# Giving each unit of split weights in the first MLP its own start address in SBUF

## The chip, the cores and the metric

The kernel runs on one core of a Trainium2 chip. The metric is the device time of one execution in microseconds (us). The kernel before took 1201.2, 1201.91 and 1201.94 us in three runs; the median is 1201.91 us.

## The reference

The program is a decoder trunk of two layers over 512 tokens of width 1024, in float32. Each layer is a mixer followed by a dense MLP with a hidden width of 4096:

```python
for layer in range(DEPTH):                      # DEPTH = 2
    h = rmsnorm(x, norm_mix_g[layer])
    mix = even_mixer(h, ...) if layer % 2 == 0 else mlstm_mixer(h, ...)
    x = x + mix
    h = rmsnorm(x, norm_mlp_g[layer])
    x = x + sqrelu_mlp(h, mlp_w1[layer], mlp_w2[layer])

def sqrelu_mlp(h, w1, w2):
    return jnp.square(jax.nn.relu(h @ w1)) @ w2
```

The even mixer runs a state-space layer beside a dilated attention; the odd one is an mLSTM in chunks. This document is about the MLP of layer 0.

## The kernel before, in words

Activations stand transposed: 128 channels on the partitions, 512 tokens along a row. Every large weight matrix is cut into units of 128 x 1024 floats: eight blocks of 128 x 128 that stand side by side in a row of 4096 bytes. A unit passes through three steps. A DMA puts it into a raw buffer `wr` (three of these). `w_pump` (line 151) then splits it: ScalarE copies it to `wh` rounded to the type fp32r (line 158), and VectorE writes the rest, raw minus `wh`, to `wl` (line 159). There are two buffers of each in the pool `wp`, and from the first MLP on a third in the pool `wp2`; units take them in turn (lines 154 to 157). Activations are split in the same way into a high and a low part, so that a product becomes three matmuls that add up in PSUM (`mm3`, line 174): `wh` with the high part, `wh` with the low part, `wl` with the high part. In each of them a 128 x 128 block of the weights is the stationary operand, which LDWEIGHTS puts into the array, and 512 columns of activations are the moving one. So a unit is worth 24 pairs of LDWEIGHTS and matmul.

The first MLP (`mlp`, line 261) uses 64 units, that is 1536 matmuls: in two halves, 16 units of `w1` (moving: the eight high and eight low tiles of `hg`) and then 16 of `w2` (moving: the tiles `sh` and `sl`, two units for one output). The order of the units is the list that `unit_list` makes (line 1272); splits are made two units ahead, in the MLP three (line 153). The second MLP (`mlp_rows`) is another function, with units of its own.

Addresses: a pool lays its buffers one after the other along a partition's row, and pools follow one another. In the program as it is allocated, all buffers of `wh` and `wl`, the buffer of `hg` and all of `sh` and `sl` start at 96 more than a multiple of 256 bytes, and since blocks are 512 bytes and tiles 2048 bytes long, so does every operand of the first MLP's products. Two other products take the weights from the same `wh` and `wl` with moving tiles that start elsewhere. In the output projection of the odd mixer (line 1227) these are `mh` and `ml`, which all start at 160 more than a multiple of 256, 64 bytes off the weights. In that of the even mixer (line 1001) they are the four 4096-byte tiles `y` at 96, and `yh` and `yl` at 224, 128 bytes off; the order of line 34 mixes the two kinds, three matmuls of one block at a time, in the order y, yh, yh, y, y, yh, y, yh of a unit's blocks.

Of the kernel before, what the change touches and what calls it, by code (L numbers as in the profile page):

```python
# [10 lines left out]
F32R = mybir.dt.float32r  # L11
# [5 lines left out]
P = 128  # L17
# [44 lines left out]
class Trunk:  # L62
# [88 lines left out]
    def w_pump(self):  # L151
        n = 0 if self.wp2 is None else 1
        self.w_dma(min(self.wi + self.AHEAD_DMA + n * self.MORE_DMA, len(self.units)))
        while self.wsx < min(self.wi + self.AHEAD_SPLIT + n, len(self.units)):
            r = self.raw.pop(self.wsx)
            third = self.wp2 is not None and self.wsx % 3 == 2
            pool, bufs = (self.wp2, 1) if third else (self.wp, 2)
            h = self.t(pool, (P, 1024), "wh", F32R, bufs)
            l = self.t(pool, (P, 1024), "wl", F32R, bufs)
            self.copy_act(h, r)  # L160
            self.sub(l, r, h.bitcast(F32))
            self.split[self.wsx] = (h, l)
            self.wsx += 1
# [97 lines left out]
    def mlp(self, nxt):  # L261
        with self.tc.tile_pool(name="mp", bufs=1) as mp:
            for half in range(2):
                s = []
                for m in range(16):
                    z = self.proj(self.hg)
                    if half == 0 and m == 1:
                        r2 = self.norm_finish_sq()
                    rr = self.tmp("rr")
                    self.act(rr, z, AF.Relu)  # L270
                    sh = self.t(mp, (P, T), f"sh{m}", F32R)
                    sl = self.t(mp, (P, T), f"sl{m}", F32R)
                    self.act(sh, rr, AF.Square)
                    sf = self.tmp("sf")
                    self.mul(sf, rr, z)
                    self.sub(sl, sf, sh.bitcast(F32))
                    s.append((sh, sl))
                for m in range(KT):
                    o = self.proj(s, first=True, last=False, ks=range(0, 8))
                    self.proj(s, acc=o, first=False, last=True, ks=range(8, 16))  # L280
                    e = self.tmp("ev", bufs=3)
                    self.mul(e, o, r2)
                    self.add(self.x[m], self.x[m], e)
                    if half == 1:
                        self.prep(m, nxt)
# [989 lines left out]
    def unit_list(self):  # L1275
        a = self.a
        units = []
        for step in EVEN_SEQ.split():
            if step[0] in "uvab":
                n = int(step[1])  # L1280
                i = {"u": n, "v": 12 + n, "a": 4 + 2 * (n % 2) + 4 * (n // 2), "b": 5 + 2 * (n % 2) + 4 * (n // 2)}[step[0]]
                units.append(a["w_l0"][i])
        units += [a["w_l0"][i] for i in range(16, 26)]
        mlp = lambda l: [a["w1"][l, h * 16 + m] if ph == 0 else a["w2"][h, m] for h in range(2) for ph in range(2) for m in range(16)]
        units += mlp(0)
        base = {"z": 0, "v": 1, "q": 9, "k": 17, "o": 25}
        units += [a["w_l1"][base[step[0]] + int(step[1:])] for step in ODD_SEQ.split() if step[0] in base]
        units += [a["w_l1"][33 + m] for m in range(8)]
        units += self.rows_units()
        return units  # L1290
# [114 lines left out]
```

## Time and profile before

| what | value |
|---|---|
| median of three runs | 1201.91 us |
| profiled execution | 1202.68 us |
| its span, first to last instruction | 1200.9 us |
| TensorE (PE) busy | 1177.3 us, 98% |
| weight loads (PEld) busy | 968.8 us, 81% |
| VectorE (DVE) busy | 736.8 us, 61% |
| ScalarE (ACT) busy | 574.4 us, 48% |
| GpSimd (POOL) busy | 65.4 us, 5% |
| granted TensorE clock | 0.996 |

The profiled execution is 0.77 us longer than the median; its span leaves 1.8 us of it outside the first and last instruction. Matmuls are pipelined: a matmul's row lasts 0.39 us, while the next one starts after 0.23 us, so that the durations overlap and the busy time of PE says little. What a matmul costs is read from the distance of starts. In a timeline the columns are start (us), duration (us), engine, line, operation, names (output, then inputs), the shape, and how many follow each other in the row.

### The profile page before, as it was taken

The numbers are of one execution on the slowest core, as the hardware profiler recorded it, in microseconds if no ns is written. First come the engines' busy times: TensorE is split into PE (matmuls) and PEld (weight loads), VectorE is DVE, ScalarE is ACT, GpSimd is POOL, SyncE is SP. The second block draws the span as 40 slices with busy tenths as digits, with TensorE's granted clock in tenths as the row PEclk, the third lists the DMA queues.
The fourth block names the chain that finished last, engine by engine and source line by source line (L and its number), as shares of the span: only waits on it lengthen the run. The fifth ranks groups of instructions, "written<-read, shape, count | busy, mean of one in ns | idle before, by whom it ended". The sixth has DMA issues, their size and how long they took to land.

```text
span 1200.9 us, 15231 instructions
## 1 busy us (share of the span) xinstructions
PE 1177.3 (98%) x5580; PEld 968.8 (81%) x5580; DVE 736.8 (61%) x1307; ACT 574.4 (48%) x1009; POOL 65.4 (5%) x122
## 2 busy tenths in 40 slices
PE   6989999999999999999999999999999999999998
PEld 5868776788888888888888888887888888888887
DVE  8799864554443344435449773874665564477796
ACT  5467777443432133423336554454344344466664
POOL 0522220000000000000010000000000000000000
PEclk9989999999999999999999999999999999999999
DMA  6434522333323333232334333321499995346664
GB/s 233 123 89 124 144 75 62 114 106 94 100 91 102 101 93 104 90 104 89 103 95 152 105 106 106 93 75 45 164 350 365 349 344 176 118 148 195 206 189 157
DMA packets 61196, 170.41 MB, mean 142 GB/s; under 512 B 15481, under 2 KB 16585, under 8 KB 61121
## 3 DMA queue, kind: packets, MB, share of 16 engines
q1 hardware_dynamic: 59904, 168.13, 42.9%
q0 software_dynamic: 1216, 1.31, 0.5%
q8 instruction: 44, 0.72, 0.3%
q14 instruction: 32, 0.25, 0.1%
HBM read 145.78 MB, written 21.53 MB: 139 GB/s over the span
## 4 chain that ended last, share of the span: by engine, by line
PE 93%; DVE 3%; ACT 2%; POOL 1%; issue 1%; DMA 0%; SPq 0%; DVEq 0%; ACTq 0%
PE acc L123 83%; PE psa L123 5%; PE psb L123 3%; DVE wl L96 1%; PE psb L902 1%; POOL rA L547 1%; ACT wh L120 0%; ACT hg L117 0%; DMA wr<-in_w_l 0%; DVE hg L108 0%; PE psb L1212 0%; PE psb L307 0%; DVE x L96 0%; DVE CG L96 0%; PE psb L653 0%
## 5 line engine op out<-in xcount | busy, mean ns | idle before, releaser
L123 PE MATMUL acc<-hg,wh 128*128 128x512 f32 x1616 | 505.8, 393 | 8.9 <-ACT hg L117 8.2
L120 ACT ACTIVATE wh<-wr 128x1024 fp32r<-128x1024 f32 x219 | 231.9, 1060 | 492.0 <-PE acc L123 401.1
L96 DVE TENSOR_TENSOR wl<-wr,wh 128x1024 fp32r<-128x1024 f32 x219 | 268.2, 1226 | 269.1 <-ACT wh L120 268.5
L123 PEld LDWEIGHTS acc<-hg,wh 128*128 128x128 f32 x1616 | 302.4, 189 | 70.8 <-ACT hg L117 8.2
L123 PE MATMUL acc<-hg,wl 128*128 128x512 f32 x808 | 316.8, 392 | 0.6 <-DVE wl L96 0.6
L123 PEld LDWEIGHTS acc<-hg,wl 128*128 128x128 f32 x808 | 152.3, 188 | 32.4 <-DVE wl L96 1.1
L123 PE MATMUL acc<-wh,sp 128*128 128x512 f32 x384 | 111.4, 389 | 0.0
L123 PE MATMUL acc<-sh,wh 128*128 128x512 f32 x256 | 99.6, 389 | 0.0
L123 PE MATMUL acc<-sl,wh 128*128 128x512 f32 x256 | 99.6, 389 | 0.0
L123 PE MATMUL acc<-sh,wl 128*128 128x512 f32 x256 | 99.6, 389 | 0.0
L123 PEld LDWEIGHTS acc<-wh,sp 128*128 128x128 f32 x384 | 72.1, 188 | 15.0
L123 PE MATMUL acc<-wh,hg 128*128 128x512 f32 x192 | 63.2, 404 | 5.5 <-ACT wh L120 5.5
L123 PE MATMUL acc<-wl,sp 128*128 128x512 f32 x192 | 67.9, 390 | 0.4 <-DVE wl L96 0.4
L123 PEld LDWEIGHTS acc<-sl,wh 128*128 128x128 f32 x256 | 48.0, 188 | 10.1
L123 PEld LDWEIGHTS acc<-sh,wl 128*128 128x128 f32 x256 | 48.0, 188 | 9.9
L123 PEld LDWEIGHTS acc<-sh,wh 128*128 128x128 f32 x256 | 48.0, 188 | 9.9
L96 DVE TENSOR_TENSOR tq<-tq,tq 128x1024 f32<-128x1024 f32 x32 | 39.1, 1223 | 20.1 <-DMA tq<-in_w2s 19.7
L123 PEld LDWEIGHTS acc<-wh,hg 128*128 128x128 f32 x192 | 37.0, 194 | 13.4 <-ACT wh L120 5.9
L120 ACT ACTIVATE sp<-s 128x256 fp32r<-128x256 f32 x112 | 44.6, 408 | 1.9 <-PE acc L123 1.3
L96 DVE TENSOR_TENSOR ev<-acc,r 128x512 f32<-128x512 f32 x16 | 11.1, 692 | 53.3 <-PE acc L123 53.3
L96 DVE TENSOR_TENSOR sp<-s,sp 128x256 fp32r<-128x256 f32 x112 | 43.5, 418 | 0.3 <-ACT sp L120 0.3
L123 PEld LDWEIGHTS acc<-wl,sp 128*128 128x128 f32 x192 | 36.0, 188 | 8.2 <-DVE wl L96 0.8
(318 smaller groups left out, 1491.5 us busy)
## 6 DMA issues: line engine op xcount, KB each, us to landing
wr<-in_w SPq DMA_DIRECT2D x96, 512.0 KB, 3.5
wr<-in_w_l SPq DMA_DIRECT2D x67, 512.0 KB, 3.5
tq<-in_w2s SPq DMA_DIRECT2D x32, 512.0 KB, 6.3
T<-tq SPq DMA_DIRECT2D x32, 512.0 KB, 5.0
wr<-T SPq DMA_DIRECT2D x32, 512.0 KB, 3.4
wr<-in_w2s SPq DMA_DIRECT2D x24, 512.0 KB, 4.0
x<-in_xT SPq DMA_DIRECT2D x16, 256.0 KB, 4.7
na<-scr SPq DMA_DIRECT2D x8, 256.0 KB, 4.3
```

What stands on the lines that cost most here:

```text
L96: return self.nc.vector.tensor_tensor(out=o, in0=x, in1=y, op=op)
L120: return self.nc.scalar.activation(o, x, AF.Copy)
L123: return self.nc.tensor.matmul(o, l, r, start=start, stop=stop)
L547: gt = lambda o, x, y, op: self.nc.gpsimd.tensor_tensor(out=o, in0=x, in1=y, op=op)
L902: self.nc.tensor.transpose(t[:, k * P:(k + 1) * P], p[:, k * P:(k + 1) * P], self.ident)
```

## The change

Each of the 64 units of the first MLP gets an offset of 5 times its number, modulo 64, in elements; that is 0, 20, 40, ... bytes modulo 256, so that every multiple of 4 bytes from 0 to 252 comes once. `wh` and `wl` of a unit have the same offset. The buffers become 256 bytes longer to make room. All other units keep offset 0.

```diff
             pool, bufs = (self.wp2, 1) if third else (self.wp, 2)
-            h = self.t(pool, (P, 1024), "wh", F32R, bufs)
-            l = self.t(pool, (P, 1024), "wl", F32R, bufs)
+            o = (5 * (self.wsx - self.first)) % 64 if self.first <= self.wsx < self.first + 64 else 0
+            h = self.t(pool, (P, 1088), "wh", F32R, bufs)[:, o:o + 1024]
+            l = self.t(pool, (P, 1088), "wl", F32R, bufs)[:, o:o + 1024]
             self.copy_act(h, r)
...
+        self.first = len(units)
         units += mlp(0)
```

The order of the instructions on every engine is the same before and after; no instruction, DMA or wait is added or removed. Because the buffers grow, everything that is allocated behind them moves up: by 1024 bytes up to and including the third pair's `wh`, and by 1536 bytes behind `wp2` (`sh`, `sl` and the whole odd layer). Both are multiples of 512, so every tile outside keeps its place modulo 256.

## Rows read from the trace of the kernel before

**Rows 1.** The page: busy time by engine; the ended-last chain by engine and line.
```profile
PE 1177.3 (98%) x5580; PEld 968.8 (81%) x5580; DVE 736.8 (61%) x1307; ACT 574.4 (48%) x1009; POOL 65.4 (5%) x122
...
PE 93%; DVE 3%; ACT 2%; POOL 1%; issue 1%; DMA 0%; SPq 0%; DVEq 0%; ACTq 0%
```

**Rows 2.** Chain that ended last, first MLP (start us, us, what).
```profile
by line: PE acc L123 99.5%; PE psb L123 0.5%
```

**Rows 3.** Busy time of each engine over the first MLP, with granted clock, DMA share.
```profile
256.00:606.00 350.00, 350.00 (x1553) 289.99 (x1553) 150.50 (x177) 115.16 (x147) 0.52 (x1) 1.00 0.31 98
```

**Rows 4.** Timeline of matmuls and weight loads in the first MLP.
```profile
560.13 0.39 PE L123 MATMUL acc<-sh,wl 128*128 128x512 f32 x1
560.13 0.19 PEld L123 LDWEIGHTS acc<-sh,wh 128*128 128x128 f32 x1
560.36 0.39 PE L123 MATMUL acc<-sh,wh 128*128 128x512 f32 x1
...
592.77 0.39 PE L123 MATMUL acc<-sh,wl 128*128 128x512 f32 x1
```

**Rows 5.** Timeline of matmuls, odd mixer's output projection.
```profile
829.33 0.39 PE L123 MATMUL acc<-mh,wh 128*128 128x512 f32 x1
829.56 0.39 PE L123 MATMUL acc<-ml,wh 128*128 128x512 f32 x1
829.79 0.39 PE L123 MATMUL acc<-mh,wl 128*128 128x512 f32 x1
830.02 0.39 PE L123 MATMUL acc<-mh,wh 128*128 128x512 f32 x1
...
835.74 0.39 PE L123 MATMUL acc<-ml,wh 128*128 128x512 f32 x1
```

**Rows 6.** Timeline of matmuls, even mixer's output projection, one unit.
```profile
245.38 0.39 PE L123 MATMUL acc<-yh,wh 128*128 128x512 f32 x1
...
250.95 0.39 PE L123 MATMUL acc<-yh,wh 128*128 128x512 f32 x1
```

**Rows 7.** Timeline of matmuls, start of the first MLP.
```profile
256.29 0.40 PE L123 MATMUL acc<-hg,wl 128*128 128x512 f32 x1
...
258.37 0.39 PE L123 MATMUL acc<-hg,wl 128*128 128x512 f32 x1
...
259.73 0.39 PE L123 MATMUL acc<-hg,wl 128*128 128x512 f32 x1
```

**Rows 8.** What wl reads or writes, 256:605 us: duration ns min/median/max.
```profile
L123 PEld LDWEIGHTS acc<-hg,wl x256: 187/188/190, 256.1 to 518.4; 128*128 128x128 f32 x128
L123 PE MATMUL acc<-hg,wl x256: 387/389/478, 256.3 to 518.6; 128*128 128x512 f32 x128
...
L96 DVE TENSOR_TENSOR wl<-wr,wh x65: 1192/1226/1226, 257.2 to 601.6; 128x1024 fp32r<-128x1024 f32 x65
```

**Rows 9.** The same of yh, 217:256 us, even mixer's output projection.
```profile
L123 PE MATMUL acc<-yh,wl x28: 390/394/404, 217.0 to 255.6; 128*128 128x512 f32 x28
```

**Rows 10.** Who waited for whom, 256:605 us (total us, times, longest).
```profile
ACT wh L120 <- PE acc L123: 199.5, 55, 4.4
DVE wl L96 <- ACT wh L120: 142.4, 47, 6.8
```

**Rows 11.** VectorE on zb at 4, 8, 12 bytes off; then hg, aligned (560:605 us).
```profile
L108 DVE SCALAR_TENSOR_TENSOR sf<-zb,cvw,sf x48: 740/746/755, 643.0 to 800.3; 128x512 f32<-128x512 f32 x48
L108 DVE SCALAR_TENSOR_TENSOR hg<-x,gain,hg x4: 743/744/747, 565.1 to 597.7; 128x512 fp32r<-128x512 f32 x4
```

## The prediction

> **What bounds the kernel now.** I read the page first: PE is busy in 98% of the span and carries 93% of the chain that ended last [rows 1]. So only what lengthens or shortens TensorE's stream, or makes it wait, can move the time. [...] DVE and ACT wait for PE and for each other (ACT 199.5 us for buffers that PE frees) [rows 10]. The first MLP is 1536 matmuls back to back. Whatever one of them gains or loses is paid 1536 times and goes to the end of the program; the change gives 63 of the 64 units (the first keeps offset 0), 63 x 24 = 1512 matmuls, another address.
>
> Next I looked for what the distance between two matmuls depends on. From 560.13 to 592.77 us there are 144 matmuls: 32.64 us / 144 = 226.7 ns each [rows 4]. The weight load for the next matmul starts with the running matmul (560.13 beside 560.13) and is over 188 ns later [rows 4, 8]: both operands are read from SBUF at the same time, and 39 ns of each matmul are left. In that stretch the start of both streams is the same modulo 256 bytes, in all three weight buffers.
>
> Two products read the same weight buffers with moving tiles elsewhere. In the odd mixer's output projection the tiles lie 64 bytes off: 28 matmuls from 829.33 to 835.74 us, 228.9 ns each [rows 5]. In the even mixer's, where tiles at distance 0 and at 128 bytes take turns, a unit's 24 matmuls take from 245.38 to 250.95 us, 232.1 ns each [rows 6]. And the first MLP itself comes out of that mixture with nine slower matmuls, 256.29 to 258.37 us, 231.1 ns each, before it falls into the steady distance (six matmuls from 258.37 to 259.73 us, 226.7 ns) [rows 7]. So the distance of matmuls depends on where the moving tile lies against the weight block, and the steady 226.7 ns is the shortest rhythm that the trace shows; it is reached where the two starts agree modulo 256, and it takes some matmuls to get there.
>
> **The change, part by part.**
>
> *Order, queues, waits.* No instruction, DMA or wait is added, removed or moved on any engine. Cost 0.
>
> *The shift of everything behind the weight buffers.* By 1024 or 1536 bytes, so that outside the first MLP every distance stays as it was modulo 256, and modulo 512 too where the moving tile meets the first pair. Since the three pairs of weight buffers differ modulo 512 against `hg` before (two pairs by 256, one by 0) and the stretch that uses all three is steady, I take 512 to be without meaning. Cost 0.
>
> *The splits write, and VectorE reads, at odd starts.* The trace shows no write of this size at such a start. Reads it does show: the convolution reads its tile `zb` 4, 8 and 12 bytes past its start, at a median of 746 ns, against 744 ns for the same instruction at the start of a tile [rows 11]. I take 0 for the instruction. Cover, should a write be slower: a unit lasts 24 x 0.2267 = 5.44 us. DVE is busy 150.5 us over 64 units, 2.35 us each, ACT 1.80 us [rows 3]; the DVE split of 1.226 us [rows 8] could double and DVE would still be idle for a third of the unit, with splits made three units ahead. It reaches PE only beyond that.
>
> *The weight load at an odd start.* It may get longer. It has 39 ns to spare per matmul (226.7 less 188, rows 4 and 8). Below that it costs nothing by itself.
>
> *The rhythm of the two streams.* This is the term that decides. In each of 63 units the weight blocks lie at a distance from the moving tile that isn't 0: 20 bytes times the unit's number, modulo 256. The trace has no row for most of these distances. The bounds: a matmul's duration follows the distance to the next (389 ns where that is 226.7), so the shortest among the first MLP's products, 387 ns [rows 8], is some 2 ns better than steady, and the longest in the mixture, 404 ns [rows 9], 15 ns worse. All 1512 at either end: -3.0 us and +22.7 us. Between them stand the three rows that are not at a steady distance of 0: 228.9, 231.1 and 232.1 ns. The nearest is the first, since there, as in a unit after the change, one distance is held for many matmuls; but it is a multiple of 64, as only three of the 63 are, and after the change each unit begins with the search for a new rhythm that the second row shows, nine matmuls of 24. So I take the mean of the three, 230.7 ns, 4.0 ns more than steady: 1512 x 4.0 ns = 6.0 us.
>
> [...]
>
> *Sum.* Profiled execution 1202.68 us, of which 1200.9 are span; + 6.0 = 1208.7 us. The profiled run is 0.77 us over the median of 1201.91, so against that median: **1207.9 us**, slower by 0.5%.
>
> **The rivals.**
>
> *A. Every distance finds the same rhythm.* The steady state would be 226.7 ns for any distance, and only the search at each change of unit is paid, or not even that. For it: the first MLP reaches it from a disturbed start within nine matmuls. Against it: the odd projection holds 228.9 ns for 28 matmuls without falling back [rows 5]. Time: with the search, 9 x 4.4 ns x 63 = 2.5 us, 1204.4 us; without, 1201.9 us.
>
> [...]
>
> *B. Other distances are better.* The trace knows only distances of 0, 64 and 128. If 226.7 ns holds waits of the two reads for each other, distances between these may hold fewer; then the change makes the kernel faster. Its place is the same 1512 matmuls; it decides as soon as the mean over the units falls below 226.7 ns. For it: single matmuls are already 2 ns shorter [rows 8]. Against it: all averages over several matmuls at other distances lie higher. Price by the shortest seen: -3.0 us, 1198.9 us.
>
> [...]
>
> *C. An odd start costs far more than an even one.* [...] Only distances that are multiples of 64 stand in the trace, so nothing speaks against it directly; the reads of VectorE, which don't care [rows 11], speak against it by analogy. Up to the longest matmul seen, +15 ns: 1201.9 + 22.7 = 1224.6 us; halfway, 1213 us.
>
> *D. The offset does nothing because the starts don't move.* The slice is taken of the buffer, and all later uses take blocks of that slice; I see no way for it.
>
> **How the numbers follow.** A change of 0.2% (2.4 us) is about what a measurement of this kernel can tell from none. Forecast, a mean of 228.9 to 232.1 ns (1205.2 to 1210.1 us, its own range): 0.50. A: 0.17, half of it with the search (1204.4 us, at the edge of slower). B: 0.13. C: 0.20. The range reaches down into A, to 1201.5, and up into C, to 1217, and leaves out B and the top of C. Slower than 1204.3 us: 0.50 + 0.20 + 0.05 of A = 0.75; within 0.2%: the rest of A and a little of B, 0.14; faster: 0.11.
>
> **What would show it.** The first MLP fills the stretch from 256 to 606 us now [rows 3]; after, its end should come about 6 us later, and everything behind it should keep its lengths. Inside, the distance of matmuls should change from unit to unit, by the unit's offset, with the first unit at 226.7 ns as before. LDWEIGHTS should stay near 188 ns, the VectorE split near 1.23 us. I am wrong if the first MLP keeps its length (A) or gets shorter (B); if the distance is high for all starts that are no multiple of 16 bytes and low for the others, it is C; if PE shows waits for ACT or DVE there, a write at an odd start costs what I put at nothing.

## The result and the profile after

The changed kernel takes 1210.61 us (median of four runs, 1210.05 to 1211.41) against 1201.93 us of the kernel before in the same comparison: a ratio of 1.0072, 95% interval 1.0055 to 1.0090. It is 8.7 us slower; 6.0 us were forecast. Here and below, times are medians; a ratio is that of the whole comparison and can differ from the quotient of two medians in the fourth place. The profiled execution took 1211.41 us, 1209.6 of them span.

The page of the changed kernel, busy time by engine and shares of the chain that ended last:

```profile
PE 1186.7 (98%) x5580; PEld 969.8 (80%) x5580; DVE 736.9 (61%) x1307; ACT 574.6 (48%) x1009; POOL 65.4 (5%) x122
...
PE 93%; DVE 3%; ACT 1%; POOL 1%; issue 1%; DMA 0%; SPq 0%; DVEq 0%; ACTq 0%
```

PE's busy time grew by 9.4 us, that of the weight loads by 1.0, of VectorE by 0.1, of ScalarE by 0.2 [rows 1]. So the same matmuls lie further apart, and nothing else is longer.

The longest piece of the chain between 254 and 622 us says where. Its columns are start (us), length (us), what, and the number of instructions; it begins after the last small matmuls of the normalisation, in the third unit of the first MLP, and ends some matmuls into the next stage (before, at that stage's first small matmuls; after, at the window's end). First the kernel before, then the changed one:

```profile
273.98 341.62 PE acc L123 x1507
```
```profile
274.09 347.99 PE acc L123 x1497
```

341.62 us / 1507 = 226.7 ns before, 347.99 / 1497 = 232.5 ns after. Over 1512 matmuls the difference of 5.8 ns is 8.7 us, the whole of the measured loss. PE is still never idle there (busy time of PE, PEld, DVE, ACT, POOL over the first MLP of the changed kernel, clock, DMA share, GB/s):

```profile
256.00:615.00 359.00, 359.00 (x1554) 290.58 (x1553) 150.56 (x178) 115.41 (x147) 0.63 (x3) 1.00 0.30 96
```

DVE and ACT are busy for as long as before [rows 3], the clock is granted in full (1.00). What wl reads or writes there (duration in ns, min/median/max):

```profile
L123 PEld LDWEIGHTS acc<-hg,wl x257: 187/188/192, 256.0 to 614.9; 128*128 128x128 f32 x129
L123 PE MATMUL acc<-hg,wl x256: 387/394/482, 256.2 to 524.9; 128*128 128x512 f32 x128
...
L96 DVE TENSOR_TENSOR wl<-wr,wh x65: 1197/1226/1230, 257.2 to 610.2; 128x1024 fp32r<-128x1024 f32 x65
```

The weight load keeps its 188 ns and the split its 1226 ns; only the matmul's duration, which follows the distance to the next, is up from 389 to 394 ns [rows 8]. Inside, each unit has a rhythm of its own. The timeline of the changed kernel at three units, offsets 120, 64 and 156 bytes:

```profile
291.27 0.39 PE L123 MATMUL acc<-hg,wl 128*128 128x512 f32 x1
...
296.03 0.40 PE L123 MATMUL acc<-hg,wl 128*128 128x512 f32 x1
...
346.53 0.40 PE L123 MATMUL acc<-sl,wh 128*128 128x512 f32 x1
...
351.43 0.39 PE L123 MATMUL acc<-sl,wh 128*128 128x512 f32 x1
...
586.70 0.42 PE L123 MATMUL acc<-sh,wh 128*128 128x512 f32 x1
586.95 0.43 PE L123 MATMUL acc<-sl,wh 128*128 128x512 f32 x1
587.22 0.41 PE L123 MATMUL acc<-sh,wl 128*128 128x512 f32 x1
587.46 0.39 PE L123 MATMUL acc<-sh,wh 128*128 128x512 f32 x1
587.69 0.40 PE L123 MATMUL acc<-sl,wh 128*128 128x512 f32 x1
587.92 0.39 PE L123 MATMUL acc<-sh,wl 128*128 128x512 f32 x1
588.15 0.42 PE L123 MATMUL acc<-sh,wh 128*128 128x512 f32 x1
...
591.08 0.42 PE L123 MATMUL acc<-sh,wh 128*128 128x512 f32 x1
```

The first pair of rows is 21 matmuls apart: 4.76 us / 21 = 226.7 ns, the rhythm of before, at a start that is no multiple of 16 bytes. The second, also 21 matmuls: 4.90 / 21 = 233.3 ns, at a multiple of 64. The third unit repeats a pattern of six, and 18 matmuls from 586.70 to 591.08 us are 243.3 ns each. Worked out in this way for the 60 units behind the small matmuls of the normalisation (the fifth to the last), three hold 226.7 ns throughout (120, 216 and 244), none is below, about half lie at 233.2 to 233.6, and two above 237 (164 and 156). By kind of start the means hardly differ: 231.4 ns for the three other multiples of 64, 232.4 for the 15 multiples of 16 (those three among them), 232.7 for the 45 that are no multiple of 16.

Two units say more than their means. The one at 192 bytes repeats 226, 229 and 232 ns, 228.8 in the mean. That is also the pattern of the odd mixer's output projection, where the weights start 64 bytes before the moving tile, which is 192 modulo 256. And the one at 132 bytes needs a search before it holds the short rhythm:

```profile
508.41 0.63 PE L123 MATMUL acc<-hg,wh 128*128 128x512 f32 x2
...
509.82 0.62 PE L123 MATMUL acc<-hg,wh 128*128 128x512 f32 x2
...
510.28 0.39 PE L123 MATMUL acc<-hg,wl 128*128 128x512 f32 x1
...
513.68 0.39 PE L123 MATMUL acc<-hg,wl 128*128 128x512 f32 x1
```

Its first six distances, to 509.82 us, are 235 ns each; the 15 from 510.28 to 513.68 us are 226.7 ns each.

Outside, nothing changed. The odd mixer's output projection of the changed kernel, 28 matmuls apart, has 6.41 us / 28 = 228.9 ns, as before [rows 5]:

```profile
838.08 0.39 PE L123 MATMUL acc<-mh,wh 128*128 128x512 f32 x1
...
844.49 0.39 PE L123 MATMUL acc<-ml,wh 128*128 128x512 f32 x1
```

### The profile page after: what moved, and what is told of

It is laid out like the page before. It is cut to its first block, busy times and chain, and to the rows that moved or that the text cites. A ratio compares the mean times of both kernels' runs of the same rounds, so it can differ in the third digit from the quotient of the medians.

```text
span 1209.6 us, 15231 instructions
## 1 busy us (share of the span) xinstructions
PE 1186.7 (98%) x5580; PEld 969.8 (80%) x5580; DVE 736.9 (61%) x1307; ACT 574.6 (48%) x1009; POOL 65.4 (5%) x122
## 4 chain that ended last, share of the span: by engine, by line
PE 93%; DVE 3%; ACT 1%; POOL 1%; issue 1%; DMA 0%; SPq 0%; DVEq 0%; ACTq 0%
PE acc L123 83%; PE psa L123 5%; PE psb L123 3%; DVE wl L96 1%; PE psb L903 1%; POOL rA L548 1%; ACT wh L120 0%; ACT hg L117 0%; DMA wr<-in_w_l 0%; DVE hg L108 0%; PE psb L1213 0%; PE psb L308 0%; DVE x L96 0%; DVE CG L96 0%; PE psb L654 0%
## 5 line engine op out<-in xcount | busy, mean ns | idle before, releaser
L96 DVE TENSOR_TENSOR wl<-wr,wh 128x1024 fp32r<-128x1024 f32 x219 | 268.1, 1226 | 276.7 <-ACT wh L120 275.1
```

Of the source, the lines that this page charges most:

```text
L96: return self.nc.vector.tensor_tensor(out=o, in0=x, in1=y, op=op)
```

## The experiments

Each is shown against the kernel before, or where the line with `o =` stands, against the changed one. The profile lines are the same piece of the chain as above.

**The shift of the other buffers alone.**

```diff
-            o = (5 * (self.wsx - self.first)) % 64 if self.first <= self.wsx < self.first + 64 else 0
+            o = 0
```

> The buffers grow and everything behind them moves as in the changed kernel, but every unit keeps offset 0. Theory (what costs is the distance, modulo 256 bytes, between the start of the weight block and of the moving tile): the distances are those of before, so the time is that of before, 1201.9 us within 1.5 us, and the matmuls of the first MLP start 226.7 ns apart. Rival (the shift of the other buffers costs): some of the 8.7 us stays, 1204 to 1210 us.

Measured: 1201.41 us against 1201.79, ratio 1.0000 (0.9991 to 1.0009).

```profile
272.70 341.62 PE acc L123 x1507
```

226.7 ns. The larger buffers and the shift of everything behind them cost nothing; the whole loss belongs to the offsets.

**One offset for all, a multiple of 64.**

```diff
+            o = 16 if self.first <= self.wsx < self.first + 64 else 0
```

> All 64 units of the first MLP at offset 64 bytes, a multiple of 16 and of 64. Theory (distance): the unit that had this offset in the changed kernel held 233.3 ns, so all 1536 matmuls should: 1536 x 6.67 ns = 10.2 us, 1212 us. Rival (an odd start, one that is no multiple of 16 bytes, is what costs): a start at a multiple of 64 is free, 1201.9 us. Rival (the change of offset from unit to unit costs): no change of offset here, 1201.9 us.

Measured: 1211.29 us against 1201.79, ratio 1.0083 (1.0069 to 1.0097).

```profile
272.65 349.55 PE acc L123 x1499
```

349.55 / 1499 = 233.2 ns: 9.5 us more, where 10.2 were expected. Neither an odd start nor a change of offset is needed for a loss larger than that of the change itself. Nor is it a matter of what ScalarE does beside it: ScalarE is busy for 39% of the time from 290 to 350 us of this run and for 19% from 350 to 430 us, while each of the 60 units behind the normalisation has the same mean of 233.2 ns.

**One offset for all, no multiple of 16.**

```diff
+            o = 30 if self.first <= self.wsx < self.first + 64 else 0
```

> All 64 units of the first MLP at offset 120 bytes, no multiple of 16. Theory (distance): the unit that had it held 227 ns, the rhythm of before, so the time is that of before, 1201.9 us within 1.5 us, and not below. Rival (an odd start costs, in the weight load or in the writes of the split): slower by up to the 8.7 us of the changed kernel, 1206 to 1212 us.

Measured: 1200.90 us against 1201.79, ratio 0.9994 (0.9985 to 1.0003).

```profile
272.18 341.60 PE acc L123 x1507
```

226.7 ns: weight loads, and the splits of ScalarE and VectorE, at a start of 120 bytes cost nothing that this run shows.

**Weights and activations moved together.** By 64 and, in a later run, by 32 bytes: a constant ahead of the pools takes 128 or 96 bytes instead of 64.

```diff
-        self.pwh = self.c((P, 4, 4), "pwh")
+        self.pwh = self.c((P, 8, 4), "pwh")[:, 0:4]     # by 64 bytes
+        self.pwh = self.c((P, 6, 4), "pwh")[:, 0:4]     # by 32 bytes
```

> A constant in front of the weight pools becomes 64 bytes longer, so that weights, activations and all that lies behind them move by 64 bytes together, in the whole program. Theory (the distance between the two streams counts, not the address): 226.7 ns in the first MLP, 228.9 in the odd output projection, as before; 1201.9 us within 1.5 us. Rival (the address of the weight block itself counts, modulo 256 bytes): weights at 64 bytes past the old place hold 233.3 ns wherever they are used, some 3500 matmuls x 6.67 ns = 23 us, 1225 us.

Measured: 1201.33 us against 1201.79, ratio 0.9999 (0.9990 to 1.0007).

```profile
273.43 341.62 PE acc L123 x1507
```

> As the shift of everything by 64 bytes, but by 32: weights and activations move together, so no distance between them changes, while every moving tile, which starts at 32 past a multiple of 64 bytes in all kernels so far, now starts at a multiple of 64. [...] Theory (only the distance between the two streams counts): 226.7 ns, 1201.9 us within 1.5 us. [...]

Measured: 1201.74 us against 1201.46, ratio 1.0000 (0.9991 to 1.0009).

```profile
274.85 341.62 PE acc L123 x1507
```

226.7 ns in both. With weights at 64 bytes past their old place, the loss of the second experiment is gone as soon as the moving tiles go along: it is the distance between the two operands that counts, not the address of either. In the run by 64 bytes the odd mixer's output projection keeps its 228.9 ns too (28 matmuls from 820.33 to 826.74 us). Nor does the moving tile's own start count: in the run by 32 bytes it lies at a multiple of 64 bytes, in the kernel before 32 past one, and the matmuls start 226.7 ns apart in both.

**Four offsets in turn.**

```diff
+            o = (0, 30, 54, 61)[(self.wsx - self.first) % 4] if self.first <= self.wsx < self.first + 64 else 0
```

> The units of the first MLP take the offsets 0, 120, 216 and 244 in turn, so that the offset changes at every unit as in the changed kernel, but each is one at which the changed kernel's trace holds 227 ns. Theory (only the distance held counts): 226.7 ns but for a short search at a change, at most nine matmuls x 4.4 ns x 63 = 2.5 us; 1202 to 1204.4 us. Rival (the change from unit to unit costs): most of 8.7 us, above 1206 us.

Measured: 1202.26 us against 1201.42, ratio 1.0003 (0.9994 to 1.0012).

```profile
272.79 341.73 PE acc L123 x1507
```

341.73 / 1507 = 226.8 ns. Another offset at each unit costs 0.1 us in this piece if the offsets are ones that hold the short rhythm. From one such offset to the next, not even the search that I had put at nine matmuls is paid.

**The worst offset for all.**

```diff
+            o = 39 if self.first <= self.wsx < self.first + 64 else 0
```

> All 64 units at offset 156, the one with the longest mean distance in the changed kernel's trace, 239.1 ns in one unit. Theory (the distance held decides, and a unit's mean is the mean of its rhythm): 1536 x 12.4 ns = 19 us, 1221 us. Rival (that unit was long for another reason, such as what DVE or ACT did then): near the mean of the changed kernel, 1211 us or less.

Measured: 1226.79 us against 1202.43, ratio 1.0204 (1.0187 to 1.0221).

```profile
274.01 348.18 PE acc L123 x1431
```

348.18 / 1431 = 243.3 ns, 24.4 us more. The unit was long because of its distance. That I expected only 19 us was an error of reading: my mean of 239.1 ns for that unit had left out distances above 260 ns as stalls, and the pattern holds one of 266 in every six; with it the unit's mean is 243.9.

**Fewer weight columns.** Offset 0; all but the first and last matmul of an output load and use only 64, 96 or 32 columns of the stationary block.

```diff
-        self.mm(acc, wh, ah, first, False)
-        self.mm(acc, wh, al, False, False)
-        self.mm(acc, wl, ah, False, last)
+        c = self.COLS                      # 64, 96 or 32 in the first MLP, 128 elsewhere
+        f, g = P if first else c, P if last else c
+        self.mm(acc[0:f], wh[:, 0:f], ah, first, False)
+        self.mm(acc[0:c], wh[:, 0:c], al, False, False)
+        self.mm(acc[0:g], wl[:, 0:g], ah, False, last)
```

> Offset 0 as before, but in the first MLP a matmul's stationary block has 64 columns instead of 128, but for the first and the last matmul of each output; the other 64 columns of these products are left out, so the output lacks them. Moving columns and the number of matmuls stay. [...]

> The same with 96 columns of 128; 32 columns of these products are left out. [...] Rival (the load plays no part): 226.7 ns, 1201.9 us, with 64 columns too.

> Offset 0; in the first MLP 32 of the 128 weight columns are loaded and used, but for the first and last matmul of each output; 96 columns of these products are left out. With 64 columns the mean distance was 230.0 ns, with 96 also about 230. [...]

Measured, one run each: 1206.88 and 1206.09 us (before: 1201.42) and 1208.41 us (before: 1202.43). The piece with 64, 96 and 32 columns:

```profile
273.57 346.19 PE acc L123 x1507
```
```profile
272.26 346.77 PE acc L123 x1507
```
```profile
272.95 348.33 PE acc L123 x1507
```

229.7, 230.1 and 231.1 ns. The loads beside `sl` (mean from 300 to 500 us) took 134, 161 and 109 ns, where 128 columns take 188 [rows 8]. Loading less made the kernel slower. That the moving stream waits for the bytes of the weight load was my estimate, and it isn't shown: a quarter of the columns doesn't bring the distance below 226.7 ns. But the rival, that the load plays no part, has fallen as well: the rhythm changed with both operands at the same addresses as before. The edit also narrows what each matmul writes (`acc[0:c]`); that it is the length of the load that changes the rhythm isn't shown apart from that.

**Half the moving columns.** As with 64 weight columns, and 256 of the 512 tokens.

```diff
-        self.mm(acc[0:f], wh[:, 0:f], ah, first, False)
-        self.mm(acc[0:c], wh[:, 0:c], al, False, False)
-        self.mm(acc[0:g], wl[:, 0:g], ah, False, last)
+        t = T if c == P else T // 2
+        u, v = T if first else t, T if last else t
+        self.mm(acc[0:f, 0:u], wh[:, 0:f], ah[:, 0:u], first, False)
+        self.mm(acc[0:c, 0:t], wh[:, 0:c], al[:, 0:t], False, False)
+        self.mm(acc[0:g, 0:v], wl[:, 0:g], ah[:, 0:v], False, last)
```

> As the run with 64 weight columns, and 256 moving columns instead of 512 (but for the first and last matmul of each output); half the tokens of these products are left out. [...]

Measured: 1039.81 us, one run (before: 1202.43). The timeline within an output, 39 matmuls apart:

```profile
333.72 0.28 PE L123 MATMUL acc<-sl,wh 128*64 128x256 f32 x1
333.72 0.13 PEld L123 LDWEIGHTS acc<-sh,wl 128*64 128x64 f32 x1
333.83 0.28 PE L123 MATMUL acc<-sh,wl 128*64 128x256 f32 x1
...
338.14 0.28 PE L123 MATMUL acc<-sl,wh 128*64 128x256 f32 x1
```

4.42 us / 39 = 113.3 ns; with 512 columns and 64 weight columns it was 229.7, 2.03 times as much. A straight line through the two, an estimate from these two runs, leaves 113.3 - (229.7 - 113.3) = -3.1 ns for a price that each matmul pays whatever it streams: none is seen. That the distance grows in proportion to the columns streamed isn't shown by it: this is one run at one distance, and a load's row lasts 0.13 us here, longer than the distance, so that another rhythm may have set in.

**The version that the distance points to.** First MLP as before; both output projections brought to distance 0.

```diff
-                self.skip(self.ap, 128)
...
         self.skip(mp, 96)
+        self.skip(ot, 192)
```

> First MLP as before (offset 0). The padding of 128 bytes ahead of the even mixer's yh and yl goes, and one of 192 bytes ahead of the odd mixer's mh and ml comes, so that all moving tiles of both output projections start at the same place modulo 256 bytes as the weights. Theory (distance): 226.7 ns in both; even 192 matmuls x 5.4 ns = 1.0 us, odd 192 x 2.2 ns = 0.4 us; 1200.4 us, the best version. Rival (these stretches wait for something else, or the moved padding costs elsewhere): 1201.9 us or more, at shorter or equal distances.

Measured: 1199.95 us against 1201.42, ratio 0.9985 (0.9976 to 0.9993). Matmuls of the two projections in this kernel, 24 and 15 apart:

```profile
244.38 0.39 PE L123 MATMUL acc<-yh,wh 128*128 128x512 f32 x1
...
249.82 0.39 PE L123 MATMUL acc<-yh,wh 128*128 128x512 f32 x1
...
828.43 0.39 PE L123 MATMUL acc<-mh,wl 128*128 128x512 f32 x1
...
831.83 0.39 PE L123 MATMUL acc<-mh,wl 128*128 128x512 f32 x1
```

5.44 us / 24 and 3.40 / 15 are 226.7 ns each, where they were 232.1 [rows 6] and 228.9 [rows 5]. The expected 1.4 us are there, and this version beats both kernels: the one before by 1.5 us (ratio clear of 1), the changed one by more than 10. Here it was the padding ahead of the moving tiles that changed, not that of the weights.

## Why the prediction was right

- *What bounds the kernel.* Right: PE's stream in the first MLP became longer and everything behind it moved by that much; no engine or transfer took anything back.
- *Order, shift of buffers, odd starts, weight load: nothing.* Right, each by a run or a row: the shift alone 1.0000, offset 120 for all 0.9994, loads 188 ns and splits 1226 ns as before.
- *The rhythm of the two streams.* That it follows the distance of the two starts was right, and shown: one distance held costs 0 or 24 us in otherwise equal programs, and moving both operands together takes it away. The term was too small, 4.0 ns where 5.8 were measured. I took the mean of three rows; the two smaller ones stood for moving tiles 64 bytes past the weights (228.9 ns, which the unit at offset 192 repeats) and for the search after a disturbance. The third, the mixture at 232.1 ns, alone would have given 8.2 us. Many distances hold 233.3 ns, and no row of before shows a distance that holds it. The upper bound was too low as well: I took 15 ns from the longest duration, and offset 156 holds 16.6 ns more than steady (243.3 against 226.7). That the mean of three rows came within 2.7 us of the measured loss was partly luck, since single distances, held for all units, cost from 0 to 24 us.
- *The search at each unit* isn't paid at every change, as I had assumed: four good offsets in turn pay nothing. Where it happens, as in the unit at 132 bytes, it is 6 x 8.3 ns = 0.05 us.
- *A, one rhythm for every distance*: refuted by offset 64 for all, which holds 233.2 ns. With as many weights loaded at another distance the same matmuls start up to 16.6 ns further apart (offset 156). What they lose there, no run shows.
- *B, better distances*: none of the 60 units is below 226.7 ns.
- *C, odd starts cost far more*: refuted by the three means above and by offset 120.
- *D, the starts don't move*: refuted by the result itself.

**Open** is why the rhythm follows the distance of the starts. The runs show that it does (226.7 ns at offsets 0 and 120, 233.2 at 64, 243.3 at 156), that it isn't in proportion to the bytes loaded (231.1 ns with 32 weight columns), and, by one run with 256 moving columns (113.3 ns against 229.7), no fixed price for each matmul. A rule that gives the rhythm from the distance I could not find.

## What to carry to other kernels

Where matmuls of 512 columns in fp32r with a weight load each run back to back and PE is the bound, read the distance of starts over some twenty matmuls in each stage, not the durations. Here the same shapes gave 226.7 ns in one place and 1 to 7% more in others (228.9 to 243.3 ns), with PE never idle there; where that is so, compare the starts of the stationary and the moving buffers modulo 256 bytes. Padding one pool so that they agree cost no time and gave 226.7 ns here in both projections where it was done; a multiple of 16 and 64 was no help by itself (offset 64 for all held 233.2 ns, 120 for all 226.7).

## What I had not expected of the hardware

Many steady distances stand on steps: 226.7, 230.0 (the unit at 100 bytes of the changed kernel), 233.3 and 243.3 ns are 34, 34.5, 35 and 36.5 times 6.67 ns, the difference between 32.64 us / 144 [rows 4] and 4.90 us / 21. Others don't, such as 228.9 ns; but there a pattern of three repeats, and its sum, 686.7 ns, is 103 steps, as the pattern of six at offset 156, 1460 ns, is 219. And a shorter weight load (32 columns instead of 128, 109 ns instead of 188, which also write fewer rows of the result) went with a slower stream, 231.1 ns against 226.7, in one run.
